# Low parts of the projection's weights kept in memory for the second half of the tokens

## The chip, the cores and the metric

One core of one Trainium2 chip runs the kernel: one execution computes one decoder layer for a sequence of 2048 tokens. The metric is the device time of an execution in microseconds, as the median of several runs. The core's engines are PE (matrix multiply), DVE (vector), ACT (scalar and activation), POOL (GpSimd) and SP, which here issues DMAs only; ACT issues DMAs too, between its own work.

## The reference

The layer normalizes x, projects it by one wide matrix, and runs two branches on slices of the result: an attention in which each query keeps its 256 best keys by an indexer's score, and a Mamba-2 scan. The branches are gated, merged, projected and added to x.

```python
h = rms_norm(x, norm_g) * (1.0 + scale) + shift
proj = h @ w_in                       # (2048, 1024) @ (1024, 10084)
(q, k, v, z_att, q_idx, k_idx, w_idx, z_ssm, xbc, dt_raw, gate_logits) = split(proj)
...
o_att = sparse_attention(rope(q), rope(k), v, rope(q_idx), rope(k_idx), w_idx) * silu(z_att)
y_att = o_att @ w_branch_att
xs, bm, cm = split(silu(causal_depthwise_conv(xbc, conv_w, conv_b)))
...
y = ssd(xs, softplus(dt_raw + dt_bias), -exp(a_log), bm, cm) + d_skip * xs
y_ssm = rms_norm(y * silu(z_ssm), ssm_norm_g) @ w_branch_ssm
x = x + gate * ((sigmoid(g_att) * y_att + sigmoid(g_ssm) * y_ssm) @ w_out)
```

## The kernel before

All products of float32 data are made of three products of rounded parts: a number is split into hi (rounded to float32r) and lo = value - hi, and `mm3` (L153 to L157) adds hi*hi, lo*hi and hi*lo in one bank of PSUM. The tokens are worked on in two halves of 1024; `h_hi` and `h_lo` of one half lie in SBUF at a time. So each slice of `w_in` is loaded and split twice, once per half, and the products of one half with a slice form a unit of work.

`split_w` (L410) makes the parts of one weight tile of 128x512: ACT casts `w_raw` to `w_hi` (L414), and the engine `w_eng` subtracts to `w_lo` (L415). `w_eng` is POOL, and DVE in the last fourteen strips of the gate logits. `w_raw` has 3 buffers, `w_hi` and `w_lo` have 8 each. Two helpers call it. `w_tok` (L418) loads eight tiles of 128 rows by 512 columns for work by tokens: queries and z_ssm, where PE multiplies a block of 128 tokens with all eight tiles, and each token block of the half after the other uses the same eight (a chunk). `w_strip` (L430) loads two tiles, each of four blocks of 128x128, for work by strips of 128 output columns: conv inputs (xbc), z_att, gate logits; PE multiplies the strip with two blocks of 512 tokens. A raw load waits on SP's queue (L425, L436) until its buffer has been read by cast and subtraction.

In order of time: the indexer's inputs, k and v of both halves; queries of the first half (to 332 us), then its xbc (to 654), z_ssm (to 857) and most of its z_att; `swap` changes the half in SBUF; xbc of the second half (to 1280), its z_ssm (to 1482), z_att (to 1593), queries (to 1766) and gate logits (to 2010); `swap` again, and gate logits of the first half (to 2268). Then the scan's tail (to 2480), the attention (to some 3030), and the output products.

Beside the projections runs background work: the top-k search (DVE counts at L586, ACT counts by signs at L618, with tiny steps on DVE between them at L597 to L600 and L627 to L630), and from 1482 us on the scan (`ssd_chunk`, with products on DVE and POOL at L977 to L1027 and its loads on SP at L946 to L955). `pump` takes as much of it after each unit as a table of credits grants. z_ssm's banks are emptied by ACT at L778. The order of instructions on every engine is then set by a scheduler that plays the program through with a model of times.

Of the kernel before, what the change touches and what calls it, by code (L numbers as in the profile page):

```python
# [22 lines left out]
F32 = mybir.dt.float32  # L23
# [6 lines left out]
OP = mybir.AluOpType  # L30
# [4 lines left out]
P = 128  # L35
# [70 lines left out]
class Layer:  # L106
    def __init__(self, ctx, tc, a, out):
        self.ctx, self.tc, self.nc, self.a, self.out = ctx, tc, tc.nc, a, out
        self.S = a["x"].shape[1]
        self.HT = self.S // 2  # L110
        self.NT = self.S // P
        self.topk = min(256, self.S // 4)
        self.dram = ctx.enter_context(tc.tile_pool(name="scratch", bufs=1, space=DRAM))
        self.const = ctx.enter_context(tc.tile_pool(name="const", bufs=1))
        self.bg, self.credit, self.done, self.ps = [], 0.0, set(), {}
        self.later = 0
        self.ahead = None


    def pump(self, us):  # L120
# [286 lines left out]
        self.h[s] = h  # L407


    def split_w(self, raw, cols=512, pool=None):  # L410
        nc, p = self.nc, pool or self.wpool
        hi = p.tile([P, 512], F32R, name="w_hi", tag="w_hi", bufs=self.wb)
        lo = p.tile([P, 512], F32R, name="w_lo", tag="w_lo", bufs=self.wb)
        nc.scalar.copy(hi[:, :cols], raw[:, :cols])  # L414
        self.w_eng.tensor_tensor(lo[:, :cols], raw[:, :cols], hi[:, :cols].bitcast(F32), op=OP.subtract)  # L415
        return hi, lo

    def w_tok(self, segs, pool=None):  # L418
        cols = sum(n for _, n in segs)
        res = []  # L420
        for k in range(KC):
            raw = self.wpool.tile([P, 512], F32, name="w_raw", tag="w_raw", bufs=RAW)
            o = 0
            for c0, n in segs:
                self.nc.sync.dma_start(raw[:, o:o + n], self.a["w_in"][0, k * P:(k + 1) * P, c0:c0 + n])  # L425
                o += n
            hi, lo = self.split_w(raw, cols, pool)
            res.append((hi[:, :cols], lo[:, :cols]))
        return res

    def w_strip(self, c0):
        res = []
        w = self.a["w_in"][0].rearrange("(k p) c -> p k c", p=P)
        for j in range(2):
            raw = self.wpool.tile([P, 512], F32, name="w_raw", tag="w_raw", bufs=RAW)
            self.nc.sync.dma_start(raw.rearrange("p (k c) -> p k c", k=4), w[:, 4 * j:4 * j + 4, c0:c0 + P])  # L436
            hi, lo = self.split_w(raw)
            for k in range(4):
                res.append((hi[:, k * P:(k + 1) * P], lo[:, k * P:(k + 1) * P]))
        return res  # L440
# [1075 lines left out]
```

## Time and profile before

| | |
|---|---|
| runs, median of 3 | 3748.47 us (3747.40 to 3749.53) |
| the profiled execution | 3743.89 us, of which the span is 3742.1 |
| granted clock of PE, mean | 0.966 of full speed |
| DMA moved | 484.12 MB, 129 GB/s over the span |
| w_lo on POOL (L415) | 276 instructions, 390.9 us busy |
| w_raw loads | 296 of 256 KB and 8 smaller ones |

The page of the profile gives busy time by engine and the costliest groups. Three more kinds of answers from its trace are used: busy time by stretch, waits (who waited for whom, in us, times and the longest), and instructions in order of time. A matmul's end is modelled, so a PE that is busy is not at its peak; the granted clock tells at which share of full speed it ran.

### The profile page before, as it was taken

What the parts mean: (1) busy time and instruction counts of PE and PEld (TensorE: products, weight loads), DVE (VectorE), ACT (ScalarE), POOL (GpSimd) and SP (SyncE); (2) the same over time, 40 slices, a digit from 0 to 9 for tenths busy, and PEclk for the clock granted to TensorE, in tenths of its full rate; (3) what the DMA queues carried; (4) which work ended last, traced back from release to release, by engine and by line L of the source; (5) the groups of instructions that cost most, each with busy time, mean ns of one, the idle gap of its engine ahead of it and who ended that gap; (6) DMA issues with size and microseconds to landing.
All of it is one profiled execution on the core that took longest, in us unless ns stands there. A gap on an engine that the chain in (4) does not pass through costs nothing. (4 is left out here: it accounts for less than half of the span.)

```text
span 3742.1 us, 50447 instructions
## 1 busy us (share of the span) xinstructions
PE 3474.2 (93%) x16497; PEld 2858.7 (76%) x16497; DVE 2713.7 (73%) x5833; ACT 1855.6 (50%) x3927; POOL 969.4 (26%) x886
## 2 busy tenths in 40 slices
PE   6999999999999999988999996579989999999999
PEld 5887877777777777776788785568878878788887
DVE  6667999958999978799666868867767743443433
ACT  3444665574674573565444544446656643433310
POOL 4112122122222122575674756700000000000000
PEclk9999999999999999998999997689999999999999
DMA  6443334223433323544556556443243144544443
GB/s 219 147 148 103 82 85 120 82 92 104 121 88 102 94 87 105 167 147 134 160 176 193 177 156 199 136 122 78 75 111 83 46 156 151 182 160 157 151 153 126
DMA packets 480060, 484.12 MB, mean 129 GB/s; under 512 B 61292, under 2 KB 341428, under 8 KB 479796
## 3 DMA queue, kind: packets, MB, share of 16 engines
q1 hardware_dynamic: 324608, 340.01, 30.6%
q10 hardware_dynamic: 155188, 140.88, 11.5%
q8 instruction: 130, 2.13, 0.3%
q14 instruction: 134, 1.10, 0.1%
HBM read 335.05 MB, written 145.72 MB: 128 GB/s over the span
## 5 line engine op out<-in xcount | busy, mean ns | idle before, releaser
L415 POOL TENSOR_TENSOR w_lo<-w_raw,w_hi 128x512 fp32r<-128x512 f32 (+1 forms) x276 | 390.9, 1425 | 1145.9 <-ACT w_hi L414 1031.3
L155 PE MATMUL mm<-h_hi,w_hi 128*128 128x512 f32 x1536 | 616.3, 401 | 8.1 <-ACT xr L821 5.5
L157 PE MATMUL mm<-h_lo,w_hi 128*128 128x512 f32 x1536 | 614.6, 400 | 1.4 <-DVE h_lo L405 1.4
L156 PE MATMUL mm<-h_hi,w_lo 128*128 128x512 f32 x1536 | 613.2, 399 | 0.0
L155 PE MATMUL mm<-w_hi,h_hi 128*128 128x512 f32 (+1 forms) x1024 | 403.1, 394 | 31.5 <-ACT ev L778 11.3
L156 PE MATMUL mm<-w_hi,h_lo 128*128 128x512 f32 (+1 forms) x1024 | 401.0, 392 | 3.1 <-DVE h_lo L378 3.0
L157 PE MATMUL mm<-w_lo,h_hi 128*128 128x512 f32 (+1 forms) x1024 | 396.9, 391 | 3.1 <-POOL w_lo L415 3.1
L1231 DVE TENSOR_TENSOR bml<-bm,bmh 128x512 fp32r<-128x512 f32 x224 | 154.5, 691 | 315.0 <-ACT bmh L1230 314.2
L1230 ACT CAST bmh<-bm 128x512 fp32r<-128x512 f32 x224 | 138.8, 621 | 422.2 <-PE br L156 180.6
L155 PEld LDWEIGHTS mm<-h_hi,w_hi 128*128 128x128 f32 x1536 | 291.3, 190 | 68.1 <-ACT xr L821 7.9
L586 DVE TENSOR_SCALAR_CACHE_REDUCE junk<-scored,cand 128x1280 uint8<-128x1280 f32 (+4 forms) x217 | 334.7, 1542 | 3.7
L157 PEld LDWEIGHTS mm<-h_lo,w_hi 128*128 128x128 f32 x1536 | 290.9, 189 | 60.4 <-DVE h_lo L405 2.3
L156 PEld LDWEIGHTS mm<-h_hi,w_lo 128*128 128x128 f32 x1536 | 290.8, 189 | 57.9
L618 ACT ACTIVATE sjunk<-scorea,scand 128x384 int8<-128x384 f32 (+3 forms) x217 | 272.1, 1254 | 102.3 <-DVE scand L627 91.7
L155 PEld LDWEIGHTS mm<-w_hi,h_hi 128*128 128x128 f32 x1024 | 196.7, 192 | 75.5 <-ACT ev L778 13.4
L414 ACT CAST w_hi<-w_raw 128x512 fp32r<-128x512 f32 (+1 forms) x304 | 185.0, 614 | 115.4 <-DMA w_raw<-in_w_in_dram 42.5
L827 DVE SCALAR_TENSOR_TENSOR cv<-xr,cb,cv 128x512 f32<-128x512 f32 x288 | 239.9, 834 | 0.5
L157 PEld LDWEIGHTS mm<-w_lo,h_hi 128*128 128x128 f32 x1024 | 196.8, 192 | 42.9 <-POOL w_lo L415 7.0
L156 PEld LDWEIGHTS mm<-w_hi,h_lo 128*128 128x128 f32 x1024 | 197.6, 193 | 38.6 <-DVE h_lo L378 3.8
L1102 DVE CUSTOM_DVE_ANT_0 as<-bg,am 128x512 f32<-128x512 f32 (+3 forms) x304 | 181.7, 619 | 42.8 <-PE bg L157 34.9
L155 PE MATMUL br<-bmh,wbh 128*128 128x512 f32 x512 | 201.0, 393 | 4.7 <-ACT bmh L1230 4.6
L979 ACT ACTIVATE se<-se,sv 128x128 f32<-128x128 f32 x512 | 158.5, 389 | 90.1 <-DVE se L977 89.9
(384 smaller groups left out, 7935.2 us busy)
## 6 DMA issues: line engine op xcount, KB each, us to landing
w_raw<-in_w_in_dram SPq DMA_DIRECT2D x296, 256.0 KB, 2.9
se<-acT SPq DMA_DIRECT2D x64, 512.0 KB, 4.1
bm<-yT SPq DMA_DIRECT2D x128, 256.0 KB, 2.6
xs<-ev ACTq DMA_DIRECT2D x64, 256.0 KB, 2.3
zs<-ev ACTq DMA_DIRECT2D x64, 256.0 KB, 2.4
sx<-xs SPq DMA_DIRECT2D x64, 256.0 KB, 3.7
sz<-zs SPq DMA_DIRECT2D x64, 256.0 KB, 3.7
yT<-yt ACTq DMA_DIRECT2D x64, 256.0 KB, 2.7
```

The costliest lines, as they stand in the source:

```text
L155: t.matmul(ps, sh, mh, start=start, stop=False)
L156: t.matmul(ps, sl, mh, start=False, stop=False)
L157: t.matmul(ps, sh, ml, start=False, stop=stop)
L414: nc.scalar.copy(hi[:, :cols], raw[:, :cols])
L415: self.w_eng.tensor_tensor(lo[:, :cols], raw[:, :cols], hi[:, :cols].bitcast(F32), op=OP.subtract)
L586: self.nc.vector.tensor_scalar(junk[:, :n], x, t, 0.0, op0=op, op1=OP.add, accum_out=cnt[:, i:i + 1])
L618: nc.scalar.activation(junk[:, :n], x, AF.Sign, scale=-1.0, bias=thr[:, i:i + 1], accum_out=sg[:, i:i + 1])
L827: nc.vector.scalar_tensor_tensor(y, xr[:, k:k + 512], self.cb[:, 24 * k + j:24 * k + j + 1], y, op0=OP.mult, op1=OP.add)
L979: nc.scalar.activation(e[:, h], e[:, h], AF.Exp, bias=nac[:, c, 8 * g + h:8 * g + h + 1], scale=-1.0)
L1102: nc.vector.tensor_tensor_reduce(s[kh][:, ko:ko + m], sp[:, :m], u["mask"][:, o:o + m], scale=HD ** -0.5, scalar=-3.4e38, op0=OP.add, op1= ...
L1230: nc.scalar.copy(hi, raw)
L1231: nc.vector.tensor_tensor(lo, raw, hi.bitcast(F32), op=OP.subtract)
```

## The change

The first time that `split_w` sees a tile with a key (its first column and its number), it subtracts as before and stores `w_lo` to a new tensor in the chip's memory, by a DMA on SP's queue. The second time, it loads `w_lo` from there, also on SP, and does not subtract. The raw tile is loaded and cast to `w_hi` both times. The tiles of the indexer and of k and v, which are used once, have no key.

```diff
-    def split_w(self, raw, cols=512, pool=None):
+    def split_w(self, raw, cols=512, pool=None, key=None):
         hi = p.tile([P, 512], F32R, name="w_hi", tag="w_hi", bufs=self.wb)
         lo = p.tile([P, 512], F32R, name="w_lo", tag="w_lo", bufs=self.wb)
+        if key in self.kept:
+            nc.sync.dma_start(lo.bitcast(F32), self.kept[key])
         nc.scalar.copy(hi[:, :cols], raw[:, :cols])
-        self.w_eng.tensor_tensor(lo[:, :cols], raw[:, :cols], hi[:, :cols].bitcast(F32), op=OP.subtract)
+        if key not in self.kept:
+            self.w_eng.tensor_tensor(lo[:, :cols], raw[:, :cols], hi[:, :cols].bitcast(F32), op=OP.subtract)
+            if key is not None:
+                self.kept[key] = self.dram.tile([P, 512], F32, name=f"wl{key[0]}_{key[1]}")
+                nc.sync.dma_start(self.kept[key], lo.bitcast(F32))
         return hi, lo
...
-            hi, lo = self.split_w(raw, cols, pool)
+            hi, lo = self.split_w(raw, cols, pool, (segs[0][0], k) if pool is None and cols == 512 else None)
...
-            hi, lo = self.split_w(raw)
+            hi, lo = self.split_w(raw, key=(c0, j))
```

In the order of instructions POOL has 160 splits in place of 276, DVE none in place of 28, and SP has 144 stores (L423 of the changed kernel) and 144 loads (L417) more. Line numbers of the changed kernel are up to 8 higher.

SP's queue in the queries of the first half (w_raw is a raw weight tile, adaw a tile of the modulation's weights). Before:

```order
L347 DMA x<-in_x_dram 128x2x1024 x4
L425 DMA w_raw<-in_w_in_dram 128x512 x8
L305 DMA adaw<-in_ada_w_dram 128x1024 x8
L425 DMA w_raw<-in_w_in_dram 128x512 x5
L436 DMA w_raw<-in_w_in_dram 128x4x128 x2
L341 DMA gate_d<-gcol 8x128
L436 DMA w_raw<-in_w_in_dram 128x4x128
```

The same place of the changed kernel (wl is the new tensor):

```order
L348 DMA x<-in_x_dram 128x2x1024 x4
L423 DMA wl_0_2654<-w_lo 128x512
L433 DMA w_raw<-in_w_in_dram 128x512
L423 DMA wl_1_2662<-w_lo 128x512
L433 DMA w_raw<-in_w_in_dram 128x512
L423 DMA wl_2_2670<-w_lo 128x512
L433 DMA w_raw<-in_w_in_dram 128x512
L423 DMA wl_3_2678<-w_lo 128x512
L433 DMA w_raw<-in_w_in_dram 128x512
L423 DMA wl_4_2686<-w_lo 128x512
L433 DMA w_raw<-in_w_in_dram 128x512
L423 DMA wl_5_2694<-w_lo 128x512
```

Each store stands ahead of the raw load that waits for the same split.

SP's queue at the second chunk of z_ssm of the second half (mask is the search's result). Before, a mask store, 24 raw loads in a row, and masks again:

```order
L425 DMA w_raw<-in_w_in_dram 128x512
L543 DMA iq<-qi_1_2361 128x4x64 x2
L425 DMA w_raw<-in_w_in_dram 128x512
L682 DMA mask_97<-sel 128x128
L425 DMA w_raw<-in_w_in_dram 128x512 x24
L682 DMA mask_102<-sel 128x512
L425 DMA w_raw<-in_w_in_dram 128x512 x3
```

The changed kernel, the eight loads of that chunk with the raw loads between:

```order
L417 DMA w_lo<-wl_0_7578 128x512
L417 DMA w_lo<-wl_1_7586 128x512
L417 DMA w_lo<-wl_2_7594 128x512
L433 DMA w_raw<-in_w_in_dram 128x512
L417 DMA w_lo<-wl_3_7602 128x512
L433 DMA w_raw<-in_w_in_dram 128x512
L417 DMA w_lo<-wl_4_7610 128x512
L433 DMA w_raw<-in_w_in_dram 128x512
L417 DMA w_lo<-wl_5_7618 128x512
L417 DMA w_lo<-wl_6_7626 128x512
L417 DMA w_lo<-wl_7_7634 128x512
L433 DMA w_raw<-in_w_in_dram 128x512 x5
```

Two or three raw loads of a chunk now stand behind its last load of w_lo.

ACT's order at the first change of chunk in z_ssm of the second half (sjunk is a count of the search, ev the eviction of mm, zs its store). Before:

```order
L618 ACTIVATE sjunk,ssg<-scorea,scand 128x1152
L414 CAST w_hi<-w_raw 128x512
L618 ACTIVATE sjunk,ssg<-scorea,scand 128x896
L414 CAST w_hi<-w_raw 128x512 x2
L618 ACTIVATE sjunk,ssg<-scorea,scand 128x1152
L618 ACTIVATE sjunk,ssg<-scorea,scand 128x896
L618 ACTIVATE sjunk,ssg<-scorea,scand 128x1152
L618 ACTIVATE sjunk,ssg<-scorea,scand 128x896
L778 ACTIVATE ev<-mm 128x512 x2
L779 DMA zs_75<-ev 128x512
L618 ACTIVATE sjunk,ssg<-scorea,scand 128x1152
L779 DMA zs_75<-ev 128x512
```

The changed kernel:

```order
L626 ACTIVATE sjunk,ssg<-scorea,scand 128x1152
L418 CAST w_hi<-w_raw 128x512
L626 ACTIVATE sjunk,ssg<-scorea,scand 128x896
L626 ACTIVATE sjunk,ssg<-scorea,scand 128x1152
L418 CAST w_hi<-w_raw 128x512 x2
L626 ACTIVATE sjunk,ssg<-scorea,scand 128x896
L786 ACTIVATE ev<-mm 128x512 x2
L787 DMA zs_75<-ev 128x512
L626 ACTIVATE sjunk,ssg<-scorea,scand 128x1152
L787 DMA zs_75<-ev 128x512
L626 ACTIVATE sjunk,ssg<-scorea,scand 128x896
L626 ACTIVATE sjunk,ssg<-scorea,scand 128x1152
```

Between the last two casts and the double eviction stood four counts of the search, and one stands there now; the casts stand later among the counts.

## Rows read from the trace of the kernel before

**Rows 1.** The page: busy time by engine, share of the span, instructions.

```profile
PE 3474.2 (93%) x16497; PEld 2858.7 (76%) x16497; DVE 2713.7 (73%) x5833; ACT 1855.6 (50%) x3927; POOL 969.4 (26%) x886
```

**Rows 2.** By stretch: us, PE, PEld, DVE, ACT, POOL busy, granted clock, DMA share, GB/s.

```profile
964.00:1280.00 316.00, 302.76 (x1403) 243.22 (x1402) 300.68 (x659) 189.75 (x350) 69.18 (x48) 1.00 0.36 100
1280.00:1482.00 202.00, 188.04 (x791) 152.22 (x790) 173.27 (x438) 116.13 (x197) 40.16 (x29) 0.96 0.27 85
...
1593.00:1766.00 173.00, 148.70 (x694) 122.10 (x693) 167.59 (x327) 97.31 (x321) 108.21 (x95) 0.88 0.44 138
...
2010.00:2268.00 258.00, 250.27 (x1254) 208.63 (x1253) 182.27 (x256) 128.78 (x334) 142.16 (x117) 0.99 0.56 177
2268.00:2480.00 212.00, 133.18 (x657) 111.68 (x656) 181.53 (x319) 104.84 (x289) 124.97 (x100) 0.71 0.53 163
```

**Rows 3.** Tile w_lo: its subtractions, ns min/median/max, first and last start.

```profile
L415 POOL TENSOR_TENSOR w_lo<-w_raw,w_hi x276: 931/1298/4858, 33.4 to 1989.0; 128x512 fp32r<-128x512 f32 x134, 128x356 fp32r<-128x356 f32 x4
L415 DVE TENSOR_TENSOR w_lo<-w_raw,w_hi x28: 685/918/1775, 2011.8 to 2210.6; 128x512 fp32r<-128x512 f32 x28
```

**Rows 4.** Lines L1003, L1004, L827: ns min/median/max; last row: 964 to 1280, mean ns.

```profile
L1003 DVE TENSOR_TENSOR sx<-sx,sy x60: 678/1117/1810, 1591.5 to 2428.0; 128x512 f32<-128x512 f32 x60
...
L1004 DVE TENSOR_TENSOR sy<-bg,sx x64: 674/691/693, 1558.5 to 2429.2; 128x512 f32<-128x512 f32 x64
...
L827 DVE SCALAR_TENSOR_TENSOR cv<-xr,cb,cv x288: 719/745/1856, 352.9 to 1291.1; 128x512 f32<-128x512 f32 x144
...
L827 DVE SCALAR_TENSOR_TENSOR cv<-xr,cb,cv 128x512 f32<-128x512 f32 x136 | 112.6, 829 | 0.2
```

**Rows 5.** DVE in order of time: start us, us, line.

```profile
1328.11 1.22 DVE L600 COPY_PREDICATED T<-accept,cand 128x2 int32<-128x2 int32 x1
...
1337.45 1.22 DVE L627 TENSOR_SCALAR scand<-sT 128x2 int32<-128x2 int32 x1
...
1341.82 0.16 DVE L600 COPY_PREDICATED T<-accept,cand 128x2 int32<-128x2 int32 x1
1341.90 0.17 DVE L627 TENSOR_SCALAR scand<-sT 128x2 int32<-128x2 int32 x1
```

**Rows 6.** Waits of PE, 1295 to 1482: us in total, times, longest.

```profile
PE mm L155 <- ACT ev L778: 8.4, 3, 3.9
PE bg L555 <- ACT relu L558: 3.9, 1, 3.9
```

**Rows 7.** By stretch, at and behind the changes of chunk; columns as in rows 2.

```profile
1335.00:1340.00 5.00, 5.00 (x23) 4.05 (x22) 4.69 (x9) 2.69 (x6) 3.09 (x3) 1.00 0.48 129
...
1345.00:1350.00 5.00, 4.79 (x14) 3.84 (x15) 4.88 (x16) 4.28 (x8) 0.00 (x0) 0.66 0.29 107
...
1395.00:1400.00 5.00, 5.00 (x13) 3.91 (x12) 0.98 (x6) 3.59 (x7) 0.00 (x0) 0.51 0.25 91
...
1445.00:1450.00 5.00, 4.21 (x9) 3.01 (x10) 5.00 (x9) 3.37 (x6) 0.00 (x0) 0.50 0.33 119
```

**Rows 8.** Waits of PE, 964 to 1280, the first and the last of six.

```profile
PE bg L555 <- ACT relu L558: 3.6, 5, 0.9
...
PE bg L556 <- DVE iql L550: 0.4, 1, 0.4
```

**Rows 9.** Longest waits of PE, 1482 to 1766 and 2010 to 2268.

```profile
PE bg L1030 <- DVE sy L1027: 10.6, 3, 6.9
...
PE bg L155 <- DVE sy L998: 4.3, 2, 2.7
```

**Rows 10.** SP's first issues (start us, us); the page's DMA issues (KB, us to landing).

```profile
0.79 2.31 SPq L305 DMA_DIRECT2D adaw<-in_ada_w_dram  x5
...
w_raw<-in_w_in_dram SPq DMA_DIRECT2D x296, 256.0 KB, 2.9
```

**Rows 11.** Waits of SP's queue, 1593 to 1766 and 964 to 1482.

```profile
SPq L946 <- PE bg L1001: 27.0, 9, 9.5
...
SPq L682 <- DVE sel L681: 81.2, 13, 32.7
```

More of the change, by code (lines that the diff above doesn't have):

```diff
@@ L117, in __init__ @@
         self.ahead = None
+        self.kept = {}
     def pump(self, us):
```

## The prediction

> **What bounds the kernel now.** I read the page's engine line first, then a table of stages, then what w_lo costs on each engine, then who TensorE waits for in the stages that the change touches. The engine line says that PE is busy for 93% of the span [rows 1], so a change pays only where PE waits, or where its clock is low after it has waited. The table of stages [rows 2] shows where that is. From 964 to 1280 us (the conv strips of the second half of the tokens, beside the top-k search) PE is busy for 302.8 of 316 us. From 1280 to 1482 (z_ssm of the second half) it is 188.0 of 202 at a granted clock of 0.96. From 1593 to 1766 (queries of the second half, beside the scan) it is 148.7 of 173 at 0.88. From 2010 to 2268 (gate logits of the first half) it is 250.3 of 258. The tail of the scan, 2268 to 2480, has no projection in it and no w_lo; the change leaves it alone. These four stretches, with z_att between 1482 and 1593, are where weights come the second time, so POOL's or DVE's subtraction goes there. Elsewhere the change only adds.
>
> The subtraction is not itself late: 276 run on POOL with a median of 1.30 us and 28 on DVE with 0.92 us [rows 3], and POOL is busy for only 69 of 316 us and 40 of 202 us in the first two stretches [rows 2], all of it w_lo. What it does cost is seen on DVE. L1003, which reads two tiles from SBUF, spreads from 678 to 1810 ns with a median of 1117 while POOL works for the scan; L1004, one of whose inputs is in PSUM, stays between 674 and 693 [rows 4]. In the conv strips, where POOL's only work is w_lo, L827 has a mean of 829 ns against a median of 745 [rows 4]: 136 x 0.084 = 11.4 us. So w_lo slows DVE, and DVE is busy for 300.7 of 316 us there [rows 2].
>
> The Trainium skill's page SBUF — State Buffer, section Who interferes with whom, says that a DVE instruction with two SBUF inputs and a GpSimd instruction that reads SBUF shut each other out whole, whichever starts second waiting. The trace agrees on who is hit (L1003 and not L1004 [rows 4]); how much of it reaches PE no page can tell.
>
> **Term 1, z_ssm of the second half.** Eight tokens' tiles use one chunk of eight weight tiles, and at the change of chunk POOL runs eight splits in a row. At the switch near 1330 us, two tiny DVE steps of the search take 1.22 us each while POOL splits, where L600 takes 0.16 just after [rows 5]. ACT has its search rounds ahead of the eviction of mm in its order, so a search that is late holds the eviction, and PE runs out of mm banks: three waits for L778, 8.4 us in all, and one of 3.9 us for L558 behind the same search [rows 6]. Behind each wait PE runs at a lower granted clock: 0.66, 0.51 and 0.50 over five microseconds each [rows 7], which loses 5 x (0.34 + 0.49 + 0.50) = 6.6 us. Together 8.4 + 3.9 + 6.6 = 18.9 us hang on this. In the changed kernel's ACT order one count of the search stands between the last casts and the double eviction, where four stood before; so both causes shrink, the slow steps and the rounds ahead of the eviction. Some counts still stand ahead, and the last casts now wait for later raw loads. I take three quarters of 18.9: **-14 us**, with ends 0 and -19.
>
> **Term 2, the conv strips.** PE's waits there are six small groups, 3.6 us the largest and 0.4 the smallest [rows 8], 12.6 us in all. DVE's relief is at least L827's 11.4 us, but most of these waits are one engine's latency (a transpose for the silu before it) and don't depend on how full DVE is. I take a third: **-4 us** (0 to -12.6).
>
> **Term 3, z_att and the queries.** PE waits most for the scan's L1027, 10.6 us in three waits [rows 9]. There POOL is busy for 108.2 of 173 us [rows 2] with the scan's own products, which stay, so little of DVE's stretch goes. **-4 us** (0 to -10.6).
>
> **Term 4, gate of the first half.** 28 splits x 0.918 = 25.7 us leave DVE [rows 3], which is busy for 182.3 of 258 us [rows 2]. PE waits for DVE's L998 for 4.3 us there [rows 9]. **-2 us** (0 to -4.3).
>
> **What is added.** 144 stores and 144 loads of 256 KB, all on SP's queue, and the order shows where. One issue on SP takes 2.31 / 5 = 0.46 us; a load of the same size lands 2.9 us after its issue [rows 10]. A store stands between a split and the load of the raw tile three places on, which waited for that split anyway; in the strips raw tiles are loaded tens of microseconds ahead, so 0.46 us is hidden. At the six token chunks of the first half (two of the queries, four of z_ssm) it isn't quite: a chunk has five raw loads behind splits, in two hops of three tiles, 2 x 0.46 = 0.9 us each, and 6 x 0.9 = 5.5 us if all of it shows. I take **+3 us**. SP already stands before the raw loads until POOL's split is done, so what is queued behind it (masks, scan loads) is held no longer than before.
>
> A load of w_lo waits until PE has let go of the buffer, eight tiles back. For strips that is four strips ahead, and 2.9 us is nothing. For tokens, tile k is let go in the last token of a chunk and needed in the next one, 24 matmuls later: at 23 matmuls in 5 us [rows 7] that is 24 x 0.217 = 5.2 us, less 0.46 + 2.9, so 1.8 us are left. They replace a cast and a split of 1.30 us that ran eight in a row. I take **+3 us** (0 to +26, below) for the six chunks of the second half. The two table loads that the changed order has less on ACT I count at nothing.
>
> **Sum.** -14 - 4 - 4 - 2 + 3 + 3 = -18 us. The profiled execution took 3743.9 us, of which 3742.1 are its span; the median of the runs is 3748.5, 4.6 above it. The same -18 gives 3726 for such a profile and **3730 us** as a median. The scheduler decides every row's place anew, but the two orders agree in how much scan is left behind the projections (15 of 64 groups in both), so I expect no large shift; I give it +-8 us in the range.
>
> **Rivals.** (a) *DVE's relief stays off the path.* For it: PE's waits in the strips are short, and ACT keeps some search rounds ahead of the eviction. Then term 1 gives -3, term 2 to 4 -3 together, and the additions +3: 3745.5 us, within what a measurement of this kernel can tell from no change (0.2%, 7.5 us).
>
> (b) *Late low parts, slower.* At a switch of token chunks the changed order sends eight w_lo loads and the five raw loads in one burst. In 1335 to 1340 the DMA engines moved 129 GB/s at a share of 0.48 [rows 7], so 269 GB/s when full: 13 x 0.262 MB / 269 GB/s = 12.7 us. Two tokens that run interleaved take 2 x 24 x 0.217 = 10.4 us. PE would wait 2.3 us and then lose some 2 us to the lower clock, 4.3 us at each of six chunks, +26 us; terms 1 and 3 are gone, terms 2 and 4 stay (-6), the first half costs +3: 3771 us. In the queries the loads also stand behind scan loads, which wait for PE's L1001 27.0 us in nine waits, the longest 9.5; in z_ssm behind masks, whose waits for L681 sum to 81.2 in 13 [rows 11]. It decides from the point where a w_lo load is issued 1.8 us late. Against it: before, the raw loads stood in the same queue and PE hardly waited for weights.
>
> The same page, section Summary: rules for kernel authors, says to reckon with 358 GB/s for transfers from HBM; by that estimate the burst takes 9.5 us, less than 10.4, and nobody waits. No stretch among these rows is full enough to decide between the two.
>
> (c) *All of it reaches PE.* If every wait in terms 1 to 4 that hangs on DVE goes whole: 18.9 + 12.6 + 10.6 + 4.3 - 6 = 40 us, 3708 us. It is what the page's rule of shutting out whole would give at its strongest. Against it: waits such as a transpose for its own input are no contention.
>
> (d) That it doesn't do what it says is out: the order has 144 stores, 144 loads, 116 splits fewer on POOL and 28 fewer on DVE.
>
> **How the numbers follow.** Forecast, 3720 to 3741: 0.48. (a) 0.23. (b) 0.17, part of it milder than 3771. (c) 0.12. Faster than 3741: 0.48 + 0.12 = 0.60; within 0.2%: 0.23; slower than 3756: 0.17. For 8 in 10 the range goes from 3708, the end of (c), to 3762, inside (b), with the 8 us of the new order in it.
>
> **What would show it.** Right: in the profile after, L827's mean near 745 ns in the second conv strips and POOL idle there; PE's waits for L778 between 1280 and 1482 down from 8.4 to under 4 us, the clock of that stage above 0.96. Wrong by (b): waits of PE for DMA w_lo at chunk changes, above all in the queries. Wrong by (a): L827 short, L778's waits as before. A first half that is more than 6 us longer up to the second conv strips would say that the stores were priced too low.

## The result, and the profile after

The changed kernel takes 3699.39 us, the median of 4 runs (3692.19 to 3704.26), against 3748.36 us before (4 runs, 3747.40 to 3749.53). The ratio is 0.988, with a 95% interval of 0.9867 to 0.9894: faster by 49 us. The forecast was 3730 us, so the sign is right, and the size is not: the gain is 2.7 times the 18 us of the sum, and the time lies under the low end of the range. The profiled execution after took 3696.6 us, 3694.8 of them its span; the one before had a span of 3742.1.

The page of the changed kernel, busy time by engine, and the line of the subtraction (group: busy us, mean ns, idle before):

```profile
PE 3452.0 (93%) x16497; PEld 2851.1 (77%) x16497; DVE 2624.4 (71%) x5805; ACT 1854.7 (50%) x3925; POOL 794.2 (21%) x770
...
L420 POOL TENSOR_TENSOR w_lo<-w_raw,w_hi 128x512 fp32r<-128x512 f32 (+1 forms) x160 | 228.3, 1435 | 621.0 <-ACT w_hi L418 571.6
```

Against [rows 1], DVE is busy for 89.3 us less with 28 instructions less. [rows 3] have these 28 at a median of 0.92 us, some 26 us; the other 63 us come from instructions that are still there and have become shorter.

To see where the time went, both traces were cut at the same places: each stage runs from the first matmul of its projection to the first of the next; the tail runs from the end of the last projection to the attention's first product with the values. The lengths below are worked out from one execution of each kernel.

| stage | before, us | after, us | difference |
|---|---|---|---|
| all of the first half of the tokens, and what lies ahead of it | 962.7 | 967.3 | +4.6 |
| conv strips, second half | 317.7 | 297.3 | -20.4 |
| z_ssm, second half | 201.6 | 183.8 | -17.8 |
| z_att, second half | 110.9 | 102.1 | -8.8 |
| queries, second half | 173.4 | 166.5 | -6.9 |
| gate logits, second half | 254.9 | 255.9 | +1.0 |
| gate logits, first half | 246.9 | 256.4 | +9.5 |
| tail of the scan | 176.0 | 171.4 | -4.6 |
| attention and output | 1298.0 | 1294.1 | -3.9 |

The two first stages of the second half hold 38 of the 47 us. Their rows, of before and then of after (us, then PE, PEld, DVE, ACT and POOL busy with their instructions, granted clock, DMA share, GB/s). Before, the conv strips:

```profile
962.70:1280.40 317.70, 304.46 (x1409) 244.66 (x1408) 302.31 (x663) 191.04 (x353) 69.33 (x49) 1.00 0.35 99
```

After, the conv strips, z_ssm, z_att and the queries:

```profile
967.30:1264.60 297.30, 297.30 (x1410) 246.75 (x1409) 270.05 (x678) 196.89 (x359) 0.00 (x0) 1.00 0.52 151
1264.60:1448.40 183.80, 181.04 (x789) 146.83 (x788) 145.03 (x407) 112.13 (x191) 0.00 (x0) 1.00 0.38 129
1448.40:1550.50 102.10, 100.13 (x477) 83.30 (x476) 79.33 (x161) 48.83 (x105) 30.17 (x27) 1.00 0.72 226
1550.50:1717.00 166.50, 144.09 (x716) 119.06 (x714) 162.79 (x335) 100.72 (x333) 105.32 (x89) 0.94 0.54 166
```

In the strips PE is now busy to the last tenth of a microsecond: its idle 13.2 us (317.70 less 304.46) are gone, and the busy time of the same matmuls is 7.2 us shorter. DVE falls from 302.31 to 270.05 us, by 32.3, although it has 15 instructions more in this cut. z_ssm has 2.8 us of idle PE in place of some 14 [rows 2], at a clock of 1.00 in place of 0.96. POOL is idle in both.

L827 (L835 now) in the changed kernel's strips, 967 to 1265 us, and the small search step that is L600 in [rows 5], over the whole execution (line, count, ns min/median/max, first and last start):

```profile
L835 DVE SCALAR_TENSOR_TENSOR cv<-xr,cb,cv 128x512 f32<-128x512 f32 x141 | 104.9, 746 | 0.2
...
L608 DVE COPY_PREDICATED T<-accept,cand x62: 149/162/167, 927.2 to 1358.5; 128x2 int32<-128x2 int32 x62
```

The mean is 746 ns, against 829 in [rows 4], and none of these 62 steps is over 167 ns, where [rows 5] show 1.22 us. PE's waits answer to [rows 6]: the view lists none at all in the strips of the changed kernel, and in z_ssm (1265 to 1448 us: total, times, longest) these three:

```profile
PE mm L156 <- ACT w_hi L418: 1.9, 2, 1.3
PE mm L158 <- DMA w_lo<-wl: 0.4, 1, 0.4
PE mm L156 <- ACT ev L786: 0.3, 1, 0.3
```

The 8.4 us for the eviction are 0.3. In z_att and the queries (1448 to 1717 us), the longest, which answer to [rows 9], and the one for a low part:

```profile
PE mm L156 <- ACT qe L772: 7.2, 1, 7.2
PE bg L989 <- DVE sy L1006: 4.7, 2, 2.8
PE bg L1038 <- DVE sy L1035: 3.0, 1, 3.0
...
PE mm L158 <- DMA w_lo<-wl: 1.7, 1, 1.7
```

Low parts that come late cost 0.4 and 1.7 us. Two stretches of the changed kernel's z_ssm in which chunks change:

```profile
1345.00:1370.00 25.00, 23.27 (x100) 18.04 (x99) 15.21 (x44) 20.41 (x37) 0.00 (x0) 1.00 0.61 200
...
1395.00:1420.00 25.00, 23.97 (x104) 18.80 (x103) 21.59 (x38) 8.94 (x15) 0.00 (x0) 1.00 0.70 232
```

The transfers bring 200 and 232 GB/s, and the clock stays at 1.00, its upper level (2.4 GHz), where [rows 7] have 0.66, 0.51 and 0.50 behind the changes of chunk.

### The profile page after: what moved, and what is told of

It is laid out like the page before. It is cut to its first block, busy times and chain, and to the rows that moved or that the text cites. A ratio compares the mean times of both kernels' runs of the same rounds, so it can differ in the third digit from the quotient of the medians.

```text
span 3694.8 us, 50784 instructions
## 1 busy us (share of the span) xinstructions
PE 3452.0 (93%) x16497; PEld 2851.1 (77%) x16497; DVE 2624.4 (71%) x5805; ACT 1854.7 (50%) x3925; POOL 794.2 (21%) x770
## 3 DMA queue, kind: packets, MB, share of 16 engines
q10 hardware_dynamic: 155188, 140.88, 11.7%
## 5 line engine op out<-in xcount | busy, mean ns | idle before, releaser
L420 POOL TENSOR_TENSOR w_lo<-w_raw,w_hi 128x512 fp32r<-128x512 f32 (+1 forms) x160 | 228.3, 1435 | 621.0 <-ACT w_hi L418 571.6
L835 DVE SCALAR_TENSOR_TENSOR cv<-xr,cb,cv 128x512 f32<-128x512 f32 x288 | 227.7, 792 | 0.5
```

The source lines that it names most:

```text
L835: nc.vector.scalar_tensor_tensor(y, xr[:, k:k + 512], self.cb[:, 24 * k + j:24 * k + j + 1], y, op0=OP.mult, op1=OP.add)
```

## The experiments

**Theory 1:** POOL's subtraction, which reads two SBUF tiles, lengthens what DVE does at the same time; DVE is so full beside the search that its lateness becomes PE's. **Theory 2:** it is no contention; the low part no longer hangs on a cast and then on POOL, and the scheduler has found a better order. Each ratio below is to the kernel before, run beside the experiment on the same chip. It took 3744.45 us beside four of them (POOL's work put back, no low parts, the stores alone, no keys for the gates), 3747.16 us beside the next four (over the raw tile, half of it, the first half's subtraction left out, both parts kept), and 3747.18 us beside the last three. A stage's length is always from the one profiled execution.

**POOL's work put back, low parts still loaded.** POOL subtracts `w_hi` and a constant into a tile that nobody reads, wherever a low part is loaded.

```diff
+        else:
+            junk = self.work.tile([P, 512], F32, name="wjunk", tag="wjunk", bufs=1).rearrange("p (a b) -> p a b", a=4)
+            nc.gpsimd.tensor_tensor(junk, hi.bitcast(F32).rearrange("p (a b) -> p a b", a=4),
+                                    self.tri[:, None, :].to_broadcast([P, 4, P]), op=OP.subtract)
```

> The changed kernel, with one subtraction on POOL put back beside each load of w_lo: it reads w_hi and a constant, and writes a tile that nobody reads. Loads and stores stay, and the raw tile is still freed by ACT's cast alone. Theory 1 (POOL's subtraction held DVE, and DVE's lateness reached PE): most of the gain goes; the conv strips of the second half take 312 to 320 us again (297 in the changed kernel, 318 before), its z_ssm 195 to 204 (184, 202), the whole 3730 to 3750. Theory 2 (the gain comes from a shorter chain of weights, cast to raw load without POOL between, and from the new order): both stretches stay within 4 us of 297 and 184, the whole 3695 to 3710.

Measured: 3776.85 us, ratio 1.0083 (1.0068 to 1.0098). The strips are 326.1 us, longer than theory 1 had them, and z_ssm is 196.8, as it had it. But the queries of the first half are 19 us longer and the strips there 7, where nothing was put back, and the whole is over both ranges. The tile takes room among the working tiles; whether that is the cause was not shown. So the total says little, and the next experiment does the same without a new tile.

**The same, over the raw tile.** The raw tile is dead once it has been cast, so POOL subtracts into it: same size, same two reads, no room.

```diff
+        else:
+            nc.gpsimd.tensor_tensor(raw[:, :512], raw[:, :512], hi[:, :512].bitcast(F32), op=OP.subtract)
```

> The changed kernel with the subtraction put back on POOL in the second half, written over the raw tile, which nobody reads afterwards. No further room in SBUF is taken, and the raw tile is freed by POOL again, as before the change. Theory 1 (POOL's subtraction is what cost): this is the kernel before plus the transfers, conv strips 315 to 321 us (318 before, 297 changed), z_ssm 195 to 204, the whole 3745 to 3758; and it is nearer to the kernel before than the run with the unread tile, whose queries of the first half took 19 us more though no such subtraction ran there. Theory 2 (order and queues): under 3715.

Measured: 3750.98 us, ratio 1.0008 (0.9998 to 1.0018). The whole gain is gone, although every product still uses the loaded low part. The strips came out 1.3 us above the expected range. The strips of this kernel, their L827 (L837 here) and POOL's work:

```profile
969.80:1292.10 322.30, 305.61 (x1409) 244.18 (x1408) 305.80 (x665) 191.15 (x353) 69.77 (x49) 1.00 0.48 138
...
L837 DVE SCALAR_TENSOR_TENSOR cv<-xr,cb,cv 128x512 f32<-128x512 f32 x137 | 119.2, 872 | 0.2
...
L425 POOL TENSOR_TENSOR w_raw<-w_raw,w_hi 128x512 f32<-128x512 f32 x49 | 70.7, 1447 | 249.5 <-ACT w_hi L418 247.3 <-DMA w_lo<-wl 2.2
```

All 49 operations of POOL feed nothing, so no matmul waits for one of them. Still, L827 is at 872 ns, DVE is busy for 305.8 us and the stretch is 25.0 us longer than in the changed kernel. PE's waits in the strips are back, 16.0 us in six groups; the three longest, and then z_ssm with its two longest waits:

```profile
PE mm L156 <- ACT xr L831: 4.9, 6, 1.6
PE bg L565 <- ACT relu L568: 3.6, 5, 0.9
PE tr L847 <- ACT cv L839: 3.3, 6, 1.0
...
1292.10:1487.10 195.00, 184.76 (x789) 149.10 (x789) 168.24 (x423) 114.98 (x197) 40.05 (x29) 0.98 0.38 125
...
PE mm L156 <- ACT w_hi L418: 5.4, 3, 2.8
PE mm L156 <- ACT ev L788: 4.2, 2, 2.9
```

Theory 2 has nothing to say to that. One thing is left to it: the next raw load into that buffer waits for POOL. Half the operation, and one that writes only, tell the two apart.

**Half of it.** The last experiment again, on 256 of the 512 columns.

```diff
+        else:
+            nc.gpsimd.tensor_tensor(raw[:, :256], raw[:, :256], hi[:, :256].bitcast(F32), op=OP.subtract)
```

> The same with the subtraction over 256 of the 512 columns, so about half of POOL's time. Theory 1: about half of the loss comes back, conv strips 303 to 312 us, z_ssm 187 to 197, the whole 3715 to 3738. If what costs were that POOL is called at all (a fixed price each), it stays as with the full one, over 3742; by theory 2 it stays at 3695 to 3710.

Measured: 3713.74 us, ratio 0.9911 (0.9895 to 0.9927). Strips 301.8 us, z_ssm 185.8; these two and the whole are just below what was expected:

```profile
971.10:1272.90 301.80, 298.81 (x1409) 246.40 (x1408) 285.32 (x671) 192.84 (x355) 44.77 (x48) 1.00 0.52 147
...
L837 DVE SCALAR_TENSOR_TENSOR cv<-xr,cb,cv 128x512 f32<-128x512 f32 x139 | 110.3, 795 | 0.2
```

DVE takes 15.3 us more than in the changed kernel and the stretch is 4.5 longer; with the whole operation DVE takes 35.8 more, and the stretch is 25.0 longer. By these two points the first 11 us cost nothing, and each one behind them costs one. The rows show why. Undisturbed PE needs 297.3 us for this stretch. DVE is idle for 15.4 us of it before (317.7 less 302.3), for 16.5 with the whole operation and for 16.5 with half of it: in these three its busy time plus some 16 us is the stretch, so DVE sets the pace. In the changed kernel that would be 270.1 + 16 = 286 us, less than PE's 297.3, and PE sets it. The point between lies at some 281 us of DVE, an estimate from these rows.

**POOL busy, but only writing.** Three fills of the dead raw tile, for longer than one subtraction.

```diff
+        else:
+            for _ in range(3):
+                nc.gpsimd.memset(raw, 0.0)
```

> The changed kernel with POOL made busy in the second half by three fills of the dead raw tile, which only write, in place of a subtraction that reads two tiles from SBUF; three fills of 128x512 are an estimated 1.6 to 2.0 us, from 0.205 us for 128x128, so POOL is at least as busy as with the subtraction. Theory 1a (DVE is held by POOL's reading): conv strips 297 to 302 us, z_ssm 184 to 188, the whole 3695 to 3712. Theory 1b (DVE is held whenever POOL works): conv strips 315 or more, the whole over 3740.

Measured: 3705.57 us, ratio 0.9889 (0.9872 to 0.9907). Its strips, L827 (L838), a small search step, and the fills:

```profile
971.60:1270.40 298.80, 297.42 (x1409) 246.61 (x1409) 275.49 (x678) 197.08 (x359) 80.13 (x148) 1.00 0.53 150
...
L838 DVE SCALAR_TENSOR_TENSOR cv<-xr,cb,cv 128x512 f32<-128x512 f32 x141 | 104.6, 744 | 0.2
...
L638 DVE TENSOR_SCALAR scand<-sT 128x2 int32<-128x2 int32 x29 | 9.0, 309 | 0.1
...
L426 POOL MEMSET w_raw<- 128x512 f32 x148 | 80.1, 543 | 218.6 <-ACT w_hi L418 212.9
```

POOL is busy for 80.1 us here, longer than the 69.8 of the subtractions, and holds the raw tile as they did; L827 stays at 744 ns and the strips at 298.8 us. So neither a busy POOL nor the held buffer costs the strips their 25 us: what is left is that POOL reads. In z_ssm it is less plain. It came out at 191.3 us, between the changed kernel's 183.8 and the 195.0 with the subtraction, and longer than expected. There the longest wait of PE is the one for `w_hi`, 5.8 us where the changed kernel has 1.9:

```profile
PE mm L156 <- ACT w_hi L418: 5.8, 3, 3.0
```

So the held raw tile, which delays the next raw load and its cast, may have a part in z_ssm. The fills also lengthen small steps (L638 has a mean of 309 ns in the strips; [rows 5] show it undisturbed at 0.17 us). Which of the two z_ssm lost by was not shown apart.

The Trainium skill's page SBUF — State Buffer, section Who interferes with whom, has a DVE instruction with two SBUF inputs contend with a GpSimd instruction that reads SBUF, not with one that only writes it. For L827 the traces agree: 872 ns beside subtractions, 744 beside fills, 746 beside nothing.

**The first half's subtraction left out, in the kernel before.** No low parts are stored or loaded; in the first half `w_hi` stands in for `w_lo` (a part of the result is left out), the second half is as before.

```diff
...
+        if key is not None and key not in self.kept:
+            self.kept[key] = True
+            return hi, hi
...
```

> The kernel before, with the subtraction left out in the first half, where w_hi takes the place of w_lo (that part of the computation is left out), and made in the second as before. No transfers are added. Theory 1: the conv strips of the first half, 321.5 us with the same work, fall to 295 to 305, its z_ssm from 203 to 185 to 198, the second half stays at 318 and 202; the whole 3705 to 3725. If the relief needs what only the second half has (the scan starting behind it), the first half falls by under 6 us.

Measured: 3700.24 us, ratio 0.9878 (0.9863 to 0.9892). Before and in this kernel, the strips of the first half:

```profile
332.40:653.90 321.50, 306.40 (x1415) 248.70 (x1413) 304.64 (x692) 185.75 (x298) 75.19 (x52) 0.99 0.35 99
```

```profile
335.40:636.90 301.50, 301.32 (x1416) 248.74 (x1415) 267.52 (x673) 189.56 (x302) 0.00 (x0) 1.00 0.39 106
```

20.0 us are gone in strips with no load of a low part, while the strips of the second half stay at 317.4 (317.7 before). So these strips gain the same 20 us in another place of the kernel and with no transfer. The rest fits less well. z_ssm of the first half is 198.7 us, 4.5 less than before and just over what was expected, and the whole is below its range. Of the 39.3 us by which this profile is shorter, 27.0 lie ahead of the second strips; the other 12.3 lie where nothing was spared, and their cause was not shown.

**No low parts in the second half.** Neither subtraction nor load, and no stores; `w_hi` stands in for `w_lo` there (a part of the result is left out).

```diff
...
+        if key in self.kept:
+            return hi, hi
...
```

> In the second half neither a subtraction nor a load of w_lo is made, and nothing is stored in the first: the product takes w_hi in the place of w_lo there, so that part of the computation is left out. It shows the gain without the price of the transfers. Theory 1: as the changed kernel in conv strips and z_ssm (297 and 184), less the 6 us that its first half and the 5 us that its gate logits with the scan's tail lost: 3685 to 3695. Theory 2: the same, so this run tells only what the 288 transfers cost; if it is under 3680 they cost more than the first half showed, and if it is over 3700 they cost nothing.

Measured: 3694.61 us, ratio 0.9862 (0.9846 to 0.9879). This is what sparing the subtraction brings with no transfer at all; the changed kernel's ratio is 0.0018 above it, some 7 us, with intervals that overlap. All 288 transfers cost about that. Up to the second strips PE, DVE and ACT have the order of the kernel before, and nothing is stored. Yet z_ssm of the first half took 206.7 us against 203.2, and everything from the first projection of k and v to the second strips 893.2 us, against 887.5 before and 893.8 in the changed kernel: with the same work in the same order such a stretch differs by some 6 us between executions.

**The stores alone.** The kernel before, with the stores and no load.

```diff
...
+        if key is not None and key not in self.kept:
+            self.kept[key] = self.dram.tile([P, 512], F32, name=f"wl{key[0]}_{key[1]}")
+            nc.sync.dma_start(self.kept[key], lo.bitcast(F32))
```

> The stores alone: the first half stores w_lo as in the changed kernel, the second half subtracts as before and loads nothing. Both theories: the first half loses what the changed kernel's lost, 4 to 8 us, nearly all in its z_ssm and z_att; the rest is as before, 3750 to 3758. Under 3745 would say that the stores' new order itself brings something.

Measured: 3751.88 us (10 runs; 13 of before), ratio 1.0021 (1.0012 to 1.0031): 7 us. In its profile the gate of the first half is 261.2 us and the tail 167.0, against 246.9 and 176.0 before: these two stages shift with no load and no spared subtraction.

**No keys for the gate logits.**

```diff
-            hi, lo = self.split_w(raw, key=(c0, j))
+            hi, lo = self.split_w(raw, key=None if c0 >= C_G else (c0, j))
```

> The changed kernel without keys for the gate logits: those 64 tiles are subtracted both times, POOL and DVE as before, and not stored. The gate logits of the first half took 9.5 us longer in the changed kernel, the tail and attention behind them 8.7 less. If the loads held the gate logits up, they take 247 us again and the whole is 3690 to 3699. If the scan only moved from the tail into the gate logits, tail and attention grow by as much and the whole stays at 3696 to 3706. If DVE's relief there was worth something, it is over 3706.

Measured: 3703.01 us, ratio 0.9885 (0.9870 to 0.9899), against 0.9880 with the keys. 32 tiles are subtracted a second time here, 28 of them on DVE and 4 on POOL. Keeping the gates' low parts brings nothing that can be measured. The gate of the first half is back at 246.3 us and the tail at 176.0.

**Both parts kept.** `w_hi` is stored and loaded too, with no raw load and no cast in the second half.

```diff
...
+        if key in self.kept:
+            nc.sync.dma_start(hi.bitcast(F32), self.kept[key][0])
+            nc.sync.dma_start(lo.bitcast(F32), self.kept[key][1])
+            return hi, lo
+        raw = raw()
...
```

> w_hi is stored too, and the second half loads both parts: no raw load and no cast there, 144 stores more. ACT loses 144 casts of 0.61 us, 88 us, and the loads behind ACT's casts go. If ACT's casts also held up PE (the two waits for w_hi at chunk changes in z_ssm, 1.7 and 1.0 us, and the evictions behind the casts), the second half gains some 5 us; the stores cost up to 7 us more in the first half. Theory 1 says nothing is left in conv strips, where no gap over 0.7 us is seen any more: 297 again. The whole 3690 to 3708.

Measured: 3720.69 us, ratio 0.9937 (0.9922 to 0.9952): half of the gain is lost, and the time is over the expected range. Why was not shown. The strips of the second half stay at 297.4 us, as expected. With twice the stores z_ssm of the first half is 218.3 us (206.5 in the changed kernel) and the strips there 329.2 (321.7). In the second half the queries are shorter (152.6 against 166.5) and z_att is longer (120.2 against 102.1).

**The store later in the order,** and the changed kernel once more beside it.

```diff
+                at = self.tc.cur_priority
+                self.tc.cur_priority = at + 60
                 nc.sync.dma_start(self.kept[key], lo.bitcast(F32))
+                self.tc.cur_priority = at
```

> The changed kernel with each store given a later place in the scheduler's order, so that where both are ready a raw load goes ahead of the store. If the 7 us that the stores alone cost come from raw loads standing behind stores at chunk changes, the first half gains 2 to 6 us against the changed kernel run beside it; if they come from the transfers themselves, nothing, within 4 us.

> The changed kernel again, on the chip of the runs beside it, for the comparison with later stores and for how much a stretch of the first half differs between two executions of one program: conv strips of the second half 296 to 299 us, z_ssm 183 to 186, the whole 3692 to 3704.

Measured: 3694.38 us, ratio 0.9858 (0.9840 to 0.9876), and 3703.54 us, 0.9877 (0.9858 to 0.9896), for the changed kernel. The intervals overlap, and the first half is as long in both (896.7 and 896.6 us from the first projection of k and v to the second strips), so the stores are not what differs: the gate of the first half is (242.9 and 257.5). Not shown to be better. The repeat gives the stages of the first profile again: strips 297.2, z_ssm 183.6, z_att 103.1, queries 164.9.

## Why the prediction was wrong in size

**Term 2 is the step that failed.** In the profiles the gain is 47.3 us, 29 more than the sum; 16.4 of them lie in term 2 and 11.7 in term 3. Term 2 bounded the strips by PE's waits, 12.6 us [rows 8], and took a third; the strips gave 20.4. There are two errors in it. The first is the bound. The view of waits counts from a matmul's end, and that end is modelled: a matmul that stands before a wait is drawn longer (0.39 us) than the distance at which matmuls follow each other (0.23 us), so the first part of each wait hides in PE's busy time. The stretches show it: idle 13.2 us and 7.2 us of shrunken busy time for the same matmuls, 20.4 together. Counted from start to start, 80 distances over 0.26 us exceed 0.227 us by 22.1 us in sum before; after, there are 44, and they exceed it by 3.8. So 12.6 was not the most that could be had. The second is the share. I judged each wait by its releaser ("a transpose for the silu before it" is latency). That group was 3.4 of the 12.6 us, not most of them, and the silu hung on DVE in its turn. In the strips ACT waited for DVE's L827, the last step before the silu (L829, now L837), before and after (us, times, longest):

```profile
ACT cv L829 <- DVE cv L827: 61.5, 24, 4.8
```

```profile
ACT cv L837 <- DVE cv L835: 7.2, 11, 1.3
```

PE's six groups of waits all went with POOL's reads, and came back with them over the raw tile, at 16.0 us. The sum that would have said so was on hand: L827's 11.4 us were taken for DVE's relief with the words "at least", and the other lines were not added up. DVE fell by 32.3 us.

A better step would have compared DVE's need with PE's: PE needs 317.7 less the 22.1 us of distances, 296 us, which the trace of before gives by itself; DVE alone was busy for 302. DVE was the bound there, and PE's busy share, stretched by the waits, hid it.

**Term 1 is near in size, and right in cause for most of it:** -14, with an end of -19; measured -17.8. The waits for L778 went from 8.4 to 0.3 us and the clock from 0.96 to 1.00, both as foretold for a right step. The kernel that subtracts over the raw tile loads the low parts too, and its z_ssm is 195.0 us: 11.2 of the 17.8 come back with POOL's work, and PE's waits for the eviction (L788 there) are 4.2 us, where the changed kernel has 0.3. At the first change of chunk its ACT order has one count between the last cast and the double eviction, like the changed kernel; at the second it has three, like the kernel before. So the new order alone did not do it, but how much of the other 6.6 us is the order's was not shown, and some of the 11.2 may be the held raw tile's.

**Term 3** was -4, with an end of -10.6; measured -15.7. That z_att gives 8.8 of them is in part bookkeeping: 19 PE instructions have moved from z_att to the queries (494 and 696 before, 475 and 715 after). The term took the waits for one line as its bound and put the clock at nothing; in the queries the clock rose from 0.88 [rows 2] to 0.94. L1027's wait (L1035 now) fell from 10.6 to 3.0 us, but a wait for L772 of 7.2 us has come. Without any low part, z_att took 110.1 us, and in the two executions of the changed kernel 102.1 and 103.1; so z_att's 8.8 us belong to the order as much as to the relief. The two stages together took 284.3 us before and 268.6 after; with the subtraction over the raw tile they took 285.9, and with the fills 277.4, both with the 494 and 696 instructions of before. So by these profiles some 8 us go with POOL's reads; how the rest divides stays open.

**Term 4** was -2. The gate of the first half is 9.5 us longer, and it holds 28 PE instructions more, which the tail has less (519 before, 491 after); the tail and attention give 8.5 back. The kernel with stores alone has the same shift, and so it is no price of the loads. The prediction's "the two orders agree in how much scan is left behind the projections" was wrong by these 28 instructions; these stages together cost 1 us more. That nothing is gained there was shown by the kernel without the gates' keys.

**The additions** were +3 and +3. The stores alone cost 7 us in runs (1.0021), so they were priced some 4 us too low. The sign that the prediction named for it, a first half over 6 us longer up to the second strips, came (6.3 us from the first projection of k and v on) but shows nothing about them: the kernel without low parts, which stores nothing, has 5.7 us of it. The loads cost what is left of some 7 us for all transfers: by these intervals not to be told from nothing.

**The rivals.** (a) fell with the first result. (b), late low parts, is refuted: PE waits 0.4 us for one in z_ssm and 1.7 in z_att and the queries, at a clock of 1.00 in the bursts shown. (c) was nearest in its mechanism, all of DVE's delay reaching PE, and was given 0.12; its 3708 us were still too high, because the 12.6 us in it were too few. The range ended where (c) did, so the fault in term 2 was its fault too.

## What to carry to other kernels

Where two engines are both nearly full in a stretch (here PE with 96% and DVE with 95%), work out what each would need undisturbed, and take the longer for the bound: in these profiles PE's busy share includes part of its waiting, and the sum of its waits was no upper bound of what could be won. An operation of POOL whose result nobody waits for was not free here, where it read SBUF beside a full DVE; sum what all of DVE's instructions lose, not one line. The answer was not in proportion: half of the operation cost a fifth of the whole.

## What the runs showed of the hardware that was not expected

- POOL's fills, which read nothing, left L827 alone (744 ns) and still lengthened DVE's 128x2 steps: L638 has a mean of 309 ns among fills, against 0.17 us undisturbed [rows 5].
- Traffic of 232 GB/s at a share of 0.70 went along with a granted clock of 1.00 and no wait of PE over 1.3 us in z_ssm.
- One subtraction of 128x512 on POOL (1447 ns) cost the strips 0.51 us of the end time each (25.0 us / 49), though nothing reads its result.
